# Stick-breaking attention: two query blocks in turn, and the total of later keys carried in one row instead of multiplied

## The chip, the cores and the metric

The kernel runs on one core of one Trainium2 chip. The metric is the device time of one execution in microseconds (us); lower is better. Engine names below are those of the profile: PE is TensorE (PEld its weight loads), DVE VectorE, ACT ScalarE, POOL GpSimd, SP the engine that issues the DMAs.

## The reference

A decoder trunk of two layers on 512 tokens of width 2048 in float32. Layer 0 is an indexer-sparse attention, layer 1 a stick-breaking attention with 16 query heads of 128 that share 4 key/value heads; each layer ends with an output projection, a LayerNorm and a gated per-layer embedding. The change lies in the stick-breaking attention:

```python
def block_fn(args):                      # one block of 128 queries
    z = jnp.einsum('bqngd,bsnd->bngqs', qg, k).astype(jnp.float32) * (HEAD_DIM ** -0.5)
    strict = key_pos[None, :] < t[:, None]
    log_om = jnp.where(strict, -jax.nn.softplus(z), 0.0)
    suffix = lax.cumsum(log_om, axis=log_om.ndim - 1, reverse=True) - log_om
    a = jnp.where(strict, jnp.exp(jax.nn.log_sigmoid(z) + suffix), 0.0)
    o = jnp.einsum('bngqs,bsnd->bqngd', a.astype(v.dtype), v)
```

The weight of key s for query t is sigmoid(z) times the product of 1 − sigmoid(z) over the keys between s and t. In log space the exponent is z minus the sum of softplus(z) over the key itself and all later ones before t.

## The kernel before, in words

Every float32 product is made of three matmuls on values split in a high and a low part (`split`: ACT rounds the high part, DVE subtracts for the low one; `mm3`: high·high, high·low, low·high). Nearly all ACT and DVE instructions go through one wrapper, so that they carry line 111 in the profile; they are told apart by their tiles. The three matmuls of `mm3` are lines 136 to 138.

The order of PE's instructions is the order in which they are written (the schedule of PE is manual); the other engines' order is made by a scheduler when the program is built, except where an instruction is pinned to program order. Each engine works through its order one by one.

The stick-breaking stage runs over four head groups g of four query heads that share a key head. `sticks(g, Q)` treats a group in ten units (i, kb): query block i of 128 queries against key block kb ≤ i of 128 keys, all four heads side by side, so that a tile has 128 keys on its partitions and 4 x 128 = 512 columns. The ten units come in the order (0,0), (1,1), (1,0), (2,2), (2,1), (2,0), (3,3) and so on: of a query block, the latest keys first. Each unit has three steps:

- `logits(u)`: three matmuls give z in one of PSUM banks 4, 5, 6, which take turns (`spare`). ACT makes e = ln(1 + exp(−|z|)) in three passes (tile `wk`), DVE makes softplus sp = max(z, 0) + e. On the diagonal (kb = i) POOL sets the keys that are not strictly earlier to zero (`strict`, line 1230). sp is split into sh and sl. For the next unit of the same query block either these parts themselves stand ready (`later`), or a running sum over the blocks so far (`run`), split into rh and rl by two further DVE operations.
- `weights(u)`: matmuls add onto z in PSUM (line 1272). With `tri`, which is −1 on and below the diagonal, minus the sum over a key and the later ones of its block; with `neg`, which is −1 everywhere, minus the sum over all later blocks of the query block (only where kb < i). ACT takes the exponential, POOL masks it on the diagonal, and it is split into two parts in the tiles `A` (shown as c).
- `values(u)`: three matmuls with V add onto the output of the query block in bank 7; after kb = 0 ACT copies it to F[g] (f<-o).

In step s stand logits(s), weights(s−1) and values(s−2). Between any two of them PE computes part of the next gate projection (tiles g, banks 0 to 3) by `interleave`, whose weights arrive by DMA (raw) and are split by ACT and DVE (wh, wl) meanwhile. At the end of a group four SiLU passes on ACT free banks 0 to 3. `split_scaled(g+1, i)` turns the queries of block i of the next group into their two parts once the present group has read block i for the last time (tiles c<-f).

Of the kernel before, what the change touches and what calls it, by code (L numbers as in the profile page):

```python
# [51 lines left out]
def steps(gen, n):  # L52
    for _ in range(n):
        next(gen, None)
# [23 lines left out]
def trunk_kernel(  # L78
# [17 lines left out]
    pe = nc.tensor  # L96
# [21 lines left out]
    act, dve, pool = (Paced(e) for e in (nc.scalar, nc.vector, nc.gpsimd))  # L118
# [9 lines left out]
    def bank(i, name="ps"):  # L128
        return psum.tile([128, 512], F32, name=name, tag=f"bank{i}")

    def split(hi, lo, src, eng=dve):
        act.activation(hi, src, AF.Copy)
        eng.tensor_tensor(lo, src, hi.bitcast(F32), ALU.subtract)

    def mm3(out, a, b, start, stop):
        pe.matmul(out, a[0], b[0], start=start, stop=False)  # L136
        pe.matmul(out, a[0], b[1], start=False, stop=False)  # L137
        pe.matmul(out, a[1], b[0], start=False, stop=stop)  # L138
# [4 lines left out]
    neg = top.tile([128, 128], F32R, name="neg")  # L143
    tri = top.tile([128, 128], F32R, name="tri")
# [19 lines left out]
    units = []  # L164
# [158 lines left out]
    bg = deque()  # L323
# [386 lines left out]
    for i in range(1, 4):  # L710
        o = (i - 1) * 128 + 64
# [493 lines left out]
    px = pc_.enter_context(ss(name="px", bufs=1))  # L1205

    def split_scaled(g, i):
        qh, ql = (q.rearrange("p (h q) -> p h q", h=4) for q in Q[i])
        src = F[g][:, :, i * 128 : (i + 1) * 128]
        act.activation(qh, src, AF.Copy, scale=HSCALE)  # L1210
        dve.scalar_tensor_tensor(ql, src, HSCALE, qh.bitcast(F32), ALU.mult, ALU.subtract)
# [11 lines left out]
        tc.keep_in_program_order(act.preload_act_table_set("natural_log_exp_and_others"))  # L1223

    def work():
        return px.tile([128, 512], F32, name="wk", tag="wk", bufs=4)

    def strict(ap):
        v = ap.rearrange("p (h q) -> p h q", h=4)
        pool.affine_select(out=v, in_=v, pattern=[[0, 4], [1, 128]], compare_op=ALU.is_gt, fill=0.0, base=0, channel_multiplier=-1)  # L1230

    def sticks(g, Q):
        units = [(i, kb) for i in range(4) for kb in range(i, -1, -1)]
        later = {}
        running = {}
        state = {}
        out = {}

        def logits(u):
            i, kb = units[u]  # L1240
            z = spare("z")
            ks = slice(kb * 128, (kb + 1) * 128)
            mm3(z, [k[:, ks] for k in K[g]], Q[i], True, True)
            e = work()
            keep = kb == i > 1
            sp = px.tile([128, 512], F32, name="run", tag="run", bufs=2) if keep else work()
            act.activation(e, z, AF.Abs)
            act.activation(e, e, AF.Exp, scale=-1.0)
            act.activation(e, e, AF.Ln, bias=1.0)
            dve.scalar_tensor_tensor(sp, z, 0.0, e, ALU.max, ALU.add)  # L1250
            if kb == i:
                strict(sp)
            parts = tuple(px.tile([128, 512], F32R, name=f"s{s}", tag=f"s{s}", bufs=4) for s in "hl")
            split(*parts, sp)
            state[u] = z, parts
            if keep:
                running[i] = sp
            if kb == i:
                later[u + 1] = parts
            elif kb:  # L1260
                below = tuple(px.tile([128, 512], F32R, name=f"r{s}", tag=f"s{s}", bufs=4) for s in "hl")
                dve.tensor_tensor(running[i], running[i], sp, ALU.add)
                dve.tensor_copy(below[0], running[i])
                dve.tensor_tensor(below[1], running[i], below[0].bitcast(F32), ALU.subtract)
                later[u + 1] = below

        def weights(u):
            i, kb = units[u]
            z, parts = state[u]
            terms = [(neg, p) for p in (later[u] if kb < i else ())] + [(tri, p) for p in parts]  # L1270
            for n, (m, p) in enumerate(terms, 1):
                pe.matmul(z, m, p, start=False, stop=n == len(terms), skip_group_check=True)  # L1272
            a = work()
            act.activation(a, z, AF.Exp)
            if kb == i:
                strict(a)
            parts = A[u % 2]
            split(*parts, a)
            state[u] = parts

        def values(u):
            i, kb = units[u]
            if kb == i:
                out[i] = bank(7, "o")
            mm3(out[i], [v[:, g * 128 : (g + 1) * 128] for v in V[kb]], state.pop(u), kb == i, kb == 0)
            if kb == 0:
                act.activation(F[g][:, :, i * 128 : (i + 1) * 128], out[i].rearrange("p (h q) -> p h q", h=4), AF.Copy)

        for s in range(12):

            done = [i for n, (i, kb) in enumerate(units) if kb == 0 and s == max(n + 3, 0 if g else 8)]
# [12 lines left out]
    def after_combining(fn, *args):  # L1304
        with tc.issue_after(combined):
            fn(*args)

    bg.extend(lambda i=i: after_combining(split_scaled, 0, i) for i in range(2))
    banks = mm_banks("g")
    chunk = gate_first(banks)  # L1310
    gemm = pumped(chunk)
    first = sticks(0, Q)
    for n in (9, 1):
        steps(gemm, n)
        steps(first, 1)
    bg.extend(lambda i=i: split_scaled(0, i) for i in (2, 3))
    steps(gemm, 8)
    gemm = pumped(chunk, 2)

    for g in range(4):  # L1320
        if g:
            log_exp()
            banks = mm_banks("g")
            gemm = pumped(gemm_w(items, plain, banks))
        if 0 < g < 3:
            bg.append(lambda g=g: split_keys(g + 1))
        if g:
            interleave(sticks(g, Q), 30 + 4, gemm, 52, lead=8)
        else:
            interleave(first, 30 - 2, gemm, 64 - 18)  # L1330
        drain()
        if g < 3:
            split_scaled(g + 1, 3)
        for h in range(4):
            sg = work()
            act.activation(sg, banks[h], AF.Silu)
            dve.tensor_tensor(F[g][:, h], F[g][:, h], sg, ALU.mult)
# [52 lines left out]
```

## Time and profile before

| what | value |
|---|---|
| median of 3 runs | 1871.95 us (1871.68 to 1872.62) |
| the profiled execution's own time | 1871.96 us |
| its span in the trace | 1870.2 us |
| first to last logits matmul of the stick-breaking stage | 1239.9 to 1480.2 us of the span |
| granted TensorE clock | 1.0 of full speed |

Busy times are unions of the intervals of an engine's instructions. A group line of the profile reads: line, engine, operation, out<-in with buffer numbers left out, shapes, count, then busy us and mean ns of one, then idle time of the engine ahead of them and what ended it. A line of the timeline reads: start, duration, engine, line, operation, operands, count.

### The profile page before, as it was taken

Reading aid. Unit: us, or ns where it says so; the run is one execution under the profiler, and the core shown is the slowest. Engines: PE = TensorE matmul, PEld = TensorE weight load, DVE = VectorE, ACT = ScalarE, POOL = GpSimd, SP = SyncE. Lnnn points to the kernel's source line nnn. Section 1 sums busy time; section 2 is a strip of 40 time slices with the busy share of each in tenths; the row PEclk is TensorE's granted clock in tenths of the full one; section 3 lists DMA queues with packets and bytes.
Section 4 is the critical chain, followed back from the end, with each engine's and each line's share of the span. In section 5 each row is a group of like instructions: output and inputs, shape, how many; then the busy total and the mean of one; then the engine's idle time right before and its main releaser. Section 6 shows DMA issues by size and latency. Waiting matters only on the chain.

```text
span 1870.2 us, 24902 instructions
## 1 busy us (share of the span) xinstructions
PE 1863.4 (100%) x9229; PEld 1586.1 (85%) x9229; DVE 1196.2 (64%) x2326; ACT 940.9 (50%) x1712; POOL 26.8 (1%) x46
## 2 busy tenths in 40 slices
PE   9999999999999999999999999999999999999998
PEld 8898888888888888888888999988888888888887
DVE  5668678566556444675467788877656645567534
ACT  3546333355554432474245444478877743347422
POOL 0000000000000000000000000000100000000000
PEclk9999999999999999999999999999999999999999
DMA  6442333322222532333334333323222253243333
GB/s 197 127 121 61 102 90 102 91 67 68 68 69 59 162 117 79 124 101 102 124 124 124 102 102 102 108 85 90 59 68 69 64 183 100 74 130 94 120 102 113
DMA packets 111178, 189.21 MB, mean 101 GB/s; under 512 B 8528, under 2 KB 29008, under 8 KB 111056
## 3 DMA queue, kind: packets, MB, share of 16 engines
q1 hardware_dynamic: 111056, 187.62, 33.1%
q8 instruction: 72, 1.18, 0.3%
q14 instruction: 50, 0.41, 0.1%
HBM read 179.21 MB, written 8.39 MB: 100 GB/s over the span
## 4 chain that ended last, share of the span: by engine, by line
PE 99%; ACT 0%; DVE 0%; issue 0%; ACTq 0%
PE g L136 12%; PE g L138 12%; PE g L137 12%; PE o L137 7%; PE o L138 7%; PE o L136 7%; PE m L136 4%; PE m L138 4%; PE m L137 4%; PE q L137 3%; PE q L136 3%; PE q L138 3%; PE k L137 2%; PE k L138 2%; PE k L136 2%; PE z L1272 2%
## 5 line engine op out<-in xcount | busy, mean ns | idle before, releaser
L111 ACT ACTIVATE wh<-raw 128x512 fp32r<-128x512 f32 (+3 forms) x685 | 397.9, 582 | 702.0 <-PE g L137 234.1
L111 DVE TENSOR_TENSOR wl<-raw,wh 128x512 fp32r<-128x512 f32 (+3 forms) x685 | 430.9, 630 | 473.7 <-ACT wh L111 458.3
L136 PE MATMUL g<-xh,wh 128*128 128x512 f32 x1024 | 403.7, 394 | 0.1
L138 PE MATMUL g<-xh,wl 128*128 128x512 f32 x1024 | 399.4, 390 | 0.0
L137 PE MATMUL g<-xl,wh 128*128 128x512 f32 x1024 | 399.4, 390 | 0.0
L138 PEld LDWEIGHTS g<-xh,wl 128*128 128x128 f32 x1024 | 192.2, 188 | 40.8
L136 PEld LDWEIGHTS g<-xh,wh 128*128 128x128 f32 x1024 | 192.4, 188 | 38.3 <-ACT wk L111 0.8
L137 PEld LDWEIGHTS g<-xl,wh 128*128 128x128 f32 x1024 | 192.5, 188 | 37.0
L138 PE MATMUL o<-xh,wl 128*128 128x512 f32 x512 | 199.3, 389 | 0.0
L137 PE MATMUL o<-xl,wh 128*128 128x512 f32 x512 | 199.2, 389 | 0.0
L136 PE MATMUL o<-xh,wh 128*128 128x512 f32 x512 | 199.2, 389 | 0.0
L138 PEld LDWEIGHTS o<-xh,wl 128*128 128x128 f32 x512 | 96.1, 188 | 20.2 <-DVE wl L111 0.3
L137 PEld LDWEIGHTS o<-xl,wh 128*128 128x128 f32 x512 | 96.1, 188 | 20.1
L136 PEld LDWEIGHTS o<-xh,wh 128*128 128x128 f32 x512 | 96.1, 188 | 19.9
L136 PE MATMUL q<-xh,wh 128*128 128x512 f32 x256 | 99.6, 389 | 0.0
L137 PE MATMUL q<-xl,wh 128*128 128x512 f32 x256 | 99.6, 389 | 0.0
L138 PE MATMUL q<-xh,wl 128*128 128x512 f32 x256 | 99.6, 389 | 0.0
L111 ACT ACTIVATE sh<-st 128x512 fp32r<-128x512 f32 x80 | 49.7, 624 | 44.4 <-DVE st L111 44.3
L111 DVE TENSOR_TENSOR sl<-st,sh 128x512 fp32r<-128x512 f32 x80 | 55.2, 691 | 13.9 <-ACT sh L111 13.9
L111 DVE TENSOR_TENSOR xl<-f,xh 128x512 fp32r<-128x512 f32 x80 | 54.3, 686 | 12.6 <-ACT f L111 12.3
L111 ACT ACTIVATE wk<-z 128x512 f32<-128x512 f32 x80 | 47.2, 590 | 23.8 <-PE z L138 16.3
L136 PEld LDWEIGHTS q<-xh,wh 128*128 128x128 f32 x256 | 48.0, 188 | 10.1
(289 smaller groups left out, 3340.1 us busy)
## 6 DMA issues: line engine op xcount, KB each, us to landing
raw<-w_in_a SPq DMA_DIRECT2D x95, 512.0 KB, 3.7
raw<-w_in_b SPq DMA_DIRECT2D x64, 512.0 KB, 3.8
raw<-w_ple_gate SPq DMA_DIRECT2D x52, 512.0 KB, 3.7
raw<-w_o_a SPq DMA_DIRECT2D x24, 512.0 KB, 3.8
raw<-w_o_b SPq DMA_DIRECT2D x24, 512.0 KB, 3.7
raw<-w_kv_b SPq DMA_DIRECT2D x16, 512.0 KB, 3.7
raw<-w_ple_gate SPq DMA_DIRECT2D x24, 256.0 KB, 2.9
f<-xT SPq DMA_DIRECT2D x4, 1024.0 KB, 6.5
```

Source lines behind the costliest of these rows:

```text
L111: ins = method(*args, **kw)
L136: pe.matmul(out, a[0], b[0], start=start, stop=False)
L137: pe.matmul(out, a[0], b[1], start=False, stop=False)
L138: pe.matmul(out, a[1], b[0], start=False, stop=stop)
L1272: pe.matmul(z, m, p, start=False, stop=n == len(terms), skip_group_check=True)
```

## The change

The total over later key blocks is no longer multiplied with `neg`. It is written into row 0 of sp, the row of the block's first key, and a second triangular matrix `tri0` has −1 in the whole of the matching row, so that the two triangular matmuls of the unit spread it over all keys. Row 0's own softplus is lost by that, so DVE puts −ln(1 + exp(z)) + z = min(z, 0) − e straight into row 0 of z. The total itself is read off after the triangular matmuls: the first row of z before them minus the first row after them goes to the next unit of the query block (`first`, tile `y`, one partition by 512 columns). On the diagonal this is the sum over the whole block; off the diagonal it is what was carried in plus the block's sum without its first key.

So that this total has time to return, the units of two query blocks alternate, and two units of one query block are two steps apart. z takes turns in banks 4 and 5, and the outputs lie in banks 6 and 7. The pool of `wk` has 5 buffers instead of 4, that of sh and sl 3 instead of 4, `run` is gone, `y` has 3. The query splits follow the new order of the blocks (block 0 last).

```diff
+    tri0 = px.tile([128, 128], F32R, name="tri0")
+    dve.tensor_copy(tri0, tri.bitcast(F32))
+    dve.tensor_copy(tri0[0:1], neg[0:1].bitcast(F32))
+
     def sticks(g, Q):
-        units = [(i, kb) for i in range(4) for kb in range(i, -1, -1)]
-        later = {}
-        running = {}
+        units = [(1, 1), (3, 3), (1, 0), (3, 2), (2, 2), (3, 1), (2, 1), (3, 0), (2, 0), (0, 0)]
+        total = {}
...
-            z = spare("z")
+            z = bank(4 + u % 2, "z")
...
             dve.scalar_tensor_tensor(sp, z, 0.0, e, ALU.max, ALU.add)
+            first = None
+            if kb:
+                first = px.tile([1, 512], F32, name="y", tag="y", bufs=3)
             if kb == i:
+                if kb:
+                    dve.tensor_copy(first, z[0:1])
                 strict(sp)
-            parts = tuple(px.tile([128, 512], F32R, name=f"s{s}", tag=f"s{s}", bufs=4) for s in "hl")
+            else:
+                if kb:
+                    dve.scalar_tensor_tensor(first, z[0:1], 0.0, e[0:1], ALU.min, ALU.subtract)
+                    dve.tensor_copy(z[0:1], first)
+                else:
+                    dve.scalar_tensor_tensor(z[0:1], z[0:1], 0.0, e[0:1], ALU.min, ALU.subtract)
+                dve.tensor_copy(sp[0:1], total.pop(i))
+            parts = tuple(px.tile([128, 512], F32R, name=f"s{s}", tag=f"s{s}", bufs=3) for s in "hl")
             split(*parts, sp)
-            state[u] = z, parts
-            if keep:
-                running[i] = sp
-            if kb == i:
-                later[u + 1] = parts
-            elif kb:
-                below = tuple(px.tile([128, 512], F32R, name=f"r{s}", tag=f"s{s}", bufs=4) for s in "hl")
-                dve.tensor_tensor(running[i], running[i], sp, ALU.add)
-                dve.tensor_copy(below[0], running[i])
-                dve.tensor_tensor(below[1], running[i], below[0].bitcast(F32), ALU.subtract)
-                later[u + 1] = below
+            state[u] = z, parts, first
 
         def weights(u):
             i, kb = units[u]
-            z, parts = state[u]
-            terms = [(neg, p) for p in (later[u] if kb < i else ())] + [(tri, p) for p in parts]
-            for n, (m, p) in enumerate(terms, 1):
-                pe.matmul(z, m, p, start=False, stop=n == len(terms), skip_group_check=True)
+            z, parts, first = state[u]
+            for n, p in enumerate(parts):
+                pe.matmul(z, tri if kb == i else tri0, p, start=False, stop=n == 1, skip_group_check=True)
+            if kb:
+                dve.tensor_tensor(first, first, z[0:1], ALU.subtract)
+                total[i] = first
             a = work()
             act.activation(a, z, AF.Exp)
...
-                out[i] = bank(7, "o")
+                out[i] = bank(7 if i in (0, 3) else 6, "o")
...
-    bg.extend(lambda i=i: after_combining(split_scaled, 0, i) for i in range(2))
+    bg.extend(lambda i=i: after_combining(split_scaled, 0, i) for i in (1, 3))
...
-    bg.extend(lambda i=i: split_scaled(0, i) for i in (2, 3))
+    bg.extend(lambda i=i: split_scaled(0, i) for i in (2, 0))
...
-            split_scaled(g + 1, 3)
+            split_scaled(g + 1, 0)
```

More of the change, by code (lines that the diff above doesn't have):

```diff
@@ L1225, in work @@
     def work():
-        return px.tile([128, 512], F32, name="wk", tag="wk", bufs=4)
+        return px.tile([128, 512], F32, name="wk", tag="wk", bufs=5)
     def strict(ap):
@@ L1244, in logits @@
             e = work()
-            keep = kb == i > 1
-            sp = px.tile([128, 512], F32, name="run", tag="run", bufs=2) if keep else work()
+            sp = work()
             act.activation(e, z, AF.Abs)
@@ L1289, in sticks @@
         for s in range(12):
-            done = [i for n, (i, kb) in enumerate(units) if kb == 0 and s == max(n + 3, 0 if g else 8)]
+            done = [i for n, (i, kb) in enumerate(units) if kb == 0 and s == max(n + 3, 0 if g else 8) and i]
             if g < 3:
```

## The prediction

> **What bounds the kernel now.** I read the page first, then the busy time by stretch over the stage that the change touches, then the groups of instructions in that stage, the waits, and last the timeline around single units.
>
> ```profile
> span 1870.2 us, 24902 instructions
> PE 1863.4 (100%) x9229; PEld 1586.1 (85%) x9229; DVE 1196.2 (64%) x2326; ACT 940.9 (50%) x1712; POOL 26.8 (1%) x46
> ...
> 1300.00:1361.00 61.00, 61.00 (x269) 50.13 (x268) 39.91 (x63) 48.44 (x87) 5.88 (x8) 1.00 0.21 62
> 1361.00:1422.00 61.00, 60.90 (x268) 49.79 (x267) 39.55 (x62) 49.77 (x88) 5.88 (x8) 1.00 0.23 68
> ...
> 1239.70:1490.50 250.80, 250.23 (x1098) 205.16 (x1097) 162.31 (x257) 202.80 (x362) 23.31 (x32) 1.00 0.24 70
> ```
>
> Columns of the last three lines: stretch and length, then busy time (and count) of PE, PEld, DVE, ACT and POOL, the granted clock, and DMA. The stick-breaking stage lies between 1239.7 and 1490.5. PE is busy all of it at full clock, so a PE instruction taken out there saves its time, and a wait put in there costs its time. 268 matmuls in 60.90 us are 0.227 us each; a matmul row of 0.39 us overlaps its neighbours, so 0.227 is the price. ACT is next (49.77 of 61 us, 82%), DVE has 39.55 (65%). The waits in this stage say how little slack PE has:
>
> ```profile
> PEld o L137 <- DVE c L111: 1.1, 3, 0.5
> PEld z L1272 <- DVE sl L111: 0.9, 2, 0.6
> ...
> PEld g L136 <- ACT wk L111: 0.8, 2, 0.5
> ```
>
> (Total, times, longest.) Nearly nothing in 250 us: whatever ACT and DVE must deliver arrives, but the 0.9 on sl shows that in two units it arrives at the last moment.
>
> **What goes.** The matmuls with neg:
>
> ```profile
> L1272 PE MATMUL z<-sh,neg 128*128 128x512 f32 x12 | 4.7, 389 | 0.0
> L1272 PE MATMUL z<-sl,neg 128*128 128x512 f32 x12 | 4.7, 389 | 0.0
> L1272 PE MATMUL z<-rh,neg 128*128 128x512 f32 x12 | 4.7, 389 | 0.0
> L1272 PE MATMUL z<-rl,neg 128*128 128x512 f32 x12 | 4.7, 389 | 0.0
> ...
> L111 DVE TENSOR_TENSOR run<-run,wk 128x512 f32<-128x512 f32 x12 | 11.0, 918 | 0.3
> L111 DVE TENSOR_TENSOR rl<-run,rh 128x512 fp32r<-128x512 f32 x12 | 8.2, 683 | 0.0
> L111 DVE CAST rh<-run 128x512 fp32r<-128x512 f32 x12 | 5.0, 420 | 0.1
> ```
>
> 48 matmuls at 0.227 us are **10.9 us** off PE, 2.7 in each of the four head groups, with no new matmul in their place. The order of all other PE instructions stays, position by position; only the unit that stands at a position is another. The three DVE groups, 24.2 us in all, lay beside PE and save nothing by themselves.
>
> **What comes on DVE.** Per group 24 operations on one partition by 512: six subtractions of z's first row, six of the form min-subtract, three copies of z's row out, three copies into it, six copies of the total into sp. No operation on one partition is in the trace. Bounds:
>
> ```profile
> L111 DVE RECIPROCAL sm<-sm 128x1 f32<-128x1 f32 x64 | 10.3, 161 | 17.7 <-ACT p L111 17.0
> L111 DVE TENSOR_TENSOR f<-rp,sw 32x512 f32<-32x512 f32 x16 | 10.9, 679 | 0.4
> ```
>
> 32 partitions by 512 cost 679 ns, as 128 by 512 do (683 above): the columns set the price, not the partitions. So I take 0.68 for the two-input forms, the upper end, and 0.42 (the CAST) for a copy within SBUF; the lower end is 0.16, a price without columns. A queue of such operations starts one every 0.6 us (below, 1399.58 to 1400.19). Per group that is 18 x 0.6 + 6 x 0.42 = 13.3 us more and 6.1 less: DVE rises from 39.55 to about 46.8 in a stretch that shrinks to 58.3 us, 80%; ACT's share becomes 85%. Neither engine becomes the bound by its sum. What counts is where the new operations stand in the chains.
>
> **What the chains lose.** In each step PE issues logits of unit u (Z), the triangular matmuls of u-1 (W) and the value matmuls of u-2 (V), with gate matmuls between. These are the rows of the third group (from 1370) around the three places that I work out.
>
> ```profile
> 1377.78 0.39 PE L1272 MATMUL z<-sh,tri 128*128 128x512 f32 x1
> 1378.01 0.39 PE L1272 MATMUL z<-sl,tri 128*128 128x512 f32 x1
> 1378.35 0.68 DVE L111 TENSOR_TENSOR sl<-wk,sh 128x512 fp32r<-128x512 f32 x1
> 1378.43 0.60 ACT L111 ACTIVATE wk<-z 128x512 f32<-128x512 f32 x1 [0.21 <-PE z L1272]
> 1378.91 0.39 PE L136 MATMUL z<-c,c 128*128 128x512 f32 x1
> 1379.16 0.64 POOL L1230 TENSOR_SCALAR_AFFINE_SELECT wk<-wk 128x512 f32<-128x512 f32 x1 [1.75 <-ACT wk L111]
> ...
> 1394.78 0.39 PE L138 MATMUL z<-c,c 128*128 128x512 f32 x1
> ...
> 1399.58 0.68 DVE L111 TENSOR_TENSOR sl<-wk,sh 128x512 fp32r<-128x512 f32 x1
> 1400.19 0.68 DVE L111 TENSOR_TENSOR wl<-raw,wh 128x512 fp32r<-128x512 f32 x1
> ...
> 1401.55 0.39 PE L1272 MATMUL z<-rh,neg 128*128 128x512 f32 x1
> 1402.00 0.39 PE L1272 MATMUL z<-sh,tri 128*128 128x512 f32 x1
> ...
> 1415.83 0.39 PE L138 MATMUL z<-c,c 128*128 128x512 f32 x1
> ...
> 1420.72 0.68 DVE L111 TENSOR_TENSOR sl<-wk,sh 128x512 fp32r<-128x512 f32 x1
> 1421.49 0.39 PE L1272 MATMUL z<-sh,tri 128*128 128x512 f32 x1
> ```
>
> *First place: bank of the third unit.* The logits now alternate between two banks where three rotated, so Z of unit 2 must wait until the exponential of unit 0 has read its bank. In the built program that exponential in turn stands behind DVE's subtraction of the same bank's first row, and in groups two to four the subtraction stands behind sl of unit 1 in DVE's queue. W of unit 0 ends at 1378.40; sl of unit 1 starts at 1378.35, so the subtraction runs from 1378.95 to about 1379.63, the exponential from 1379.67 to 1380.27 (it ran from 1378.43 before), and Z of unit 2 starts at 1380.3 instead of 1378.91. **1.4 us per group**, and behind it waits all of PE's queue. In the first group the subtraction stands ahead of sl, which makes it some 0.9 there; I keep 1.4, since that group also carries the restoring copies of the x blocks.
>
> The Trainium skill, PSUM — Partial Sum Buffer, "PSUM bank collisions raise a hardware error", says that ScalarE and VectorE must not touch one bank and quadrant at once, reads against reads included, so that the two have to be put in order. That is what speaks against reading a row and the whole bank after the same matmul; the waits in the built program agree with it, and no run so far shows its price. If they could read side by side, this place would cost some 0.7 less per group and the next 0.5 less, which puts the sum some 5 us lower.
>
> *Second place: the total's way into the triangular product.* A unit off the diagonal now waits between sp and its rounding sh for one or two further DVE operations on row 0: the min-subtract (0.6) and the copy of the total (0.42), 1.0 to 1.1 us with the hand-over. At the sixth position now: last Z at 1394.78, sl done at 1400.26, 5.48 us later; the tri matmul that needs sh comes 7.22 us after Z, and that with sl 0.23 later. Of this allowance 0.45 go with the unit's own neg matmuls and 0.45 with those of the unit before: 6.55 remain to the second. The need grows by 1.1 and by about 0.7 for the exponential of the unit before, which now holds ACT's queue until its subtraction is done, ahead of sh: 7.3. That is **0.8 us of stall**. The other five off-diagonal positions come out, by the same subtraction, between nothing and 0.3, because three of them lost run, rh and rl (2.0 us) out of the DVE queue ahead of sl, and those of the last key block have no subtraction. I take 0.6 for the five: **1.4 per group**. Bounds: nothing, if the slack that the waits view does not show is there everywhere; six times 0.8.
>
> *Third place: the last unit.* Its tri matmul comes 5.66 us after the last Z (1415.83 to 1421.49). Both neg pairs ahead of it go: 4.76, and 4.98 for the one with sl. Now sl is done 5.57 us after Z. The unit that stands there after the change is (0,0), a diagonal one, which sends sp through POOL first (0.64, and some 0.1 for the hand-over): 6.3. **1.3 us per group.** The waits ahead of it stay the same, so this place is the surest.
>
> **Sum.** New stalls 1.4 + 1.4 + 1.3 = 4.1 per group, 16.4 in four. Stalls of now that fall together with them, from the two rows of waits on c and sl: 2.0, of which I take 1.5 off. Query splits: block 0 is now split last instead of block 3, and the second unit of the next group needs block 3; it is split some ten us ahead, so nothing, but one conversion more on ACT ahead of the silu that frees the gate banks, where PE already waited 0.8 in two places: 0.5 more in all. The copies that make tri0 (two in all) stand where DVE combines the last product; the first logits wait for the query split just behind: below 0.3, taken as nothing. SP's queue, its DMAs and POOL's 32 selections stay. So −10.9 + 16.4 − 1.5 + 0.5 = **+4.5 us**. The profiled execution took 1871.96 us, equal to the median 1871.95, so the forecast is **1876.5 us**: slightly slower, just over the 0.2% (3.7 us) that a measurement can tell from no change. Its own range, with each place off by a third: 1871 to 1882. Chance 0.5.
>
> **Rivals.**
> - *Faster: only the unavoidable part stalls.* If DVE and ACT reach each new operation at once, the first place costs 0.85 (subtraction from 1378.42, exponential to 1379.72) and the second nothing. For the third, the bare links are
>
> ```profile
> L111 ACT ACTIVATE wk<-wk 128x512 f32<-128x512 f32 x80 | 50.2, 627 | 1.5
> L111 ACT ACTIVATE wk<-z 128x512 f32<-128x512 f32 x80 | 47.2, 590 | 23.8 <-PE z L138 16.3 <-PE z L1272 7.3
> ...
> L111 DVE SCALAR_TENSOR_TENSOR wk<-z,wk 128x512 f32<-128x512 f32 x32 | 22.1, 689 | 19.2 <-ACT wk L111 19.0
> L111 DVE TENSOR_TENSOR sl<-wk,sh 128x512 fp32r<-128x512 f32 x32 | 21.9, 685 | 3.4 <-ACT sh L111 3.4
> ...
> L111 ACT ACTIVATE sh<-wk 128x512 fp32r<-128x512 f32 x32 | 19.9, 622 | 1.3 <-DVE wk L111 0.9 <-POOL wk L1230 0.4
> ```
>
> the matmul's 0.39, abs 0.59, exp and ln 1.25, sp 0.69, select 0.64, sh 0.62, sl 0.69, together 4.9, and some 0.3 of hand-overs: 5.2 against 4.98 leaves 0.3 to 0.6. That is 1.3 a group, 5.2 in all: −10.9 − 1.5 + 5.2 = −7.2, **1864.8 us**. For it: the order of DVE and ACT has been made anew for this program, and a PE that stalls gives both engines time. Against it: in the built order sl of unit 1 and a weight split stand ahead of those very operations. It decides where the stalls stay under 2.3 us a group. Cheaper row operations (0.16) would lead here too. Chance 0.27.
> - *Clearly slower: ACT becomes the pace.* Six exponentials per group hold ACT for the subtraction, 0.7 each, 4.2 us; with 49.8 of 58.3 us ACT has 8.5 left, most of it where PE has not yet delivered Z. If the delays add up instead of hiding in these gaps, each of the six off-diagonal units pays the 0.8 of the sixth: 1.4 + 4.8 + 1.3 = 7.5 per group, 30 in all: +18, **1890 us** at worst, 1885 with half of it hidden. Chance 0.18.
> - *The change brings nothing because PE's time is not the sum of its matmuls.* If the neg matmuls ran where PE would have waited anyway, their removal gives nothing and the stalls still come. Against it: the four neg groups show no idle time before them. Chance 0.05; 1880 to 1887.
>
> **How the numbers follow.** The forecast's own range lies a little over half above 1875.7 and the rest within 0.2%; the first rival is mostly below 1868.2. So faster 0.26, same 0.23, slower 0.51. The range takes the first rival's time and the middle of the second: 1864 to 1886.
>
> **What would show it.** In the profile after: no neg rows and 48 PE instructions fewer; small DVE groups y, z and wk of 1x512 at 0.6 to 0.7 us; in the waits, PE or PEld z waiting for ACT (the third unit) at 1 us or more four times, PEld z waiting for DVE sl at the last unit four times. The stage from first to last z would be some 245 + 16 − 11 us long, a few us longer than now. I am wrong if PE's waits in the stage stay under 9 us (then it is faster), if the 1x512 operations take 0.2 us, or if the exponentials do not wait for DVE.

## The result, and the profile after

The changed kernel takes **1884.7 us** (1884.61 to 1884.78, four runs) against 1871.86 us (1871.68 to 1872.62, four runs) of the kernel before: a ratio of 1.0068, with a 95% interval of 1.005 to 1.0085. It is 12.8 us slower where 4.5 were forecast. The profiled execution took 1884.70 us.

Two lines of the page of after, and then the busy time by stretch over the whole stage (columns as in the prediction):

```profile
span 1883.0 us, 24868 instructions
...
PE 1861.9 (99%) x9181; PEld 1575.2 (84%) x9181; DVE 1225.8 (65%) x2388; ACT 945.1 (50%) x1712; POOL 28.2 (1%) x46
```

```profile
1239.70:1503.00 263.30, 248.52 (x1050) 194.03 (x1049) 192.16 (x319) 207.17 (x362) 24.72 (x32) 1.00 0.22 66
```

The 48 matmuls are gone (9229 to 9181), yet the stage takes 263.3 us instead of 250.8, and PE has no row in 14.8 of them, where it had none in 0.6. The clock is full as before. DVE is busy 73% and ACT 79% of the stage, so neither became the bound by its sum.

The groups of the new operations on one partition, in the stage:

```profile
L111 DVE TENSOR_TENSOR y<-y,z 1x512 f32<-1x512 f32 x24 | 16.1, 672 | 8.2 <-PE z L1278 8.2
...
L111 DVE COPY wk<-y 1x512 f32<-1x512 f32 x24 | 10.0, 416 | 0.0
...
L111 DVE COPY z<-y 1x512 f32<-1x512 f32 x12 | 8.1, 674 | 0.0
```

With three more groups of 12, of 669 to 683 ns, these are 96 operations and 58.4 us. Anything that touches PSUM costs 0.67 to 0.68 us, copies too; only the copy from y into wk within SBUF costs 0.42. The waits of the stage (total, times, longest):

```profile
PEld z L1278 <- DVE sl L111: 11.7, 18, 1.4
PEld z L136 <- ACT wk L111: 9.8, 8, 2.0
DVE y L111 <- PE z L1278: 8.2, 12, 1.5
ACT wk L111 <- DVE y L111: 7.9, 11, 1.3
...
PE z L136 <- ACT wk L111: 6.9, 5, 1.6
...
PE z L1278 <- DVE sl L111: 4.6, 10, 1.1
```

The first row answers to the 0.9 us of before: PE's triangular matmuls now wait for sl 18 times. The rows with ACT wk are the logits that wait until an exponential has read their bank, and the two rows with y show why that is late: the subtraction waits for the triangular matmuls, the exponential for the subtraction.

A busy share hides part of PE's stalls, since a matmul's row lasts 0.39 or 0.50 us and the next should start 0.227 after it. So I add up by how much neighbouring starts in the stage lie further apart than 0.227 (without the places where one record is missing). That gives PE's stalls by place: 2.2 us before, **24.7 us after**. 22.5 more stalls less 10.9 us of matmuls make +11.6; the remaining 1.2 of the 12.8 lies outside the gaps counted so. In the rest, Z2 is the first logits matmul of the group's third unit, W9 the triangular matmuls of the last unit (units are counted from 0), V9 its value matmuls. This is Z2 in the third group, on the timeline of after:

```profile
1383.87 0.67 DVE L111 COPY y<-z 1x512 f32<-1x512 f32 x1
1384.02 1.61 POOL L1230 TENSOR_SCALAR_AFFINE_SELECT wk<-wk 128x512 f32<-128x512 f32 x1 [1.85 <-DVE wk L111]
...
1384.47 0.67 DVE L111 TENSOR_TENSOR sl<-wk,sh 128x512 fp32r<-128x512 f32 x1
...
1385.65 0.39 PE L1278 MATMUL z<-sl,tri 128*128 128x512 f32 x1
...
1385.67 0.63 ACT L111 ACTIVATE sh<-wk 128x512 fp32r<-128x512 f32 x1 [0.32 <-POOL wk L1230]
...
1386.33 0.69 DVE L111 TENSOR_TENSOR sl<-wk,sh 128x512 fp32r<-128x512 f32 x1 [0.15 <-ACT sh L111]
1386.94 0.67 DVE L111 TENSOR_TENSOR y<-y,z 1x512 f32<-1x512 f32 x1
1387.64 0.60 ACT L111 ACTIVATE wk<-z 128x512 f32<-128x512 f32 x1 [1.34 <-DVE y L111]
...
1388.30 0.50 PE L136 MATMUL z<-c,c 128*128 128x512 f32 x1 [1.58 <-ACT wk L111]
...
1388.63 0.40 PE L137 MATMUL z<-c,c 128*128 128x512 f32 x1
```

The triangular matmuls of unit 0 end at 1386.04. DVE then still has sl of unit 1 to do, subtracts at 1386.94, ACT takes the exponential at 1387.64, and PE's logits start at 1388.30; without the stall they were due about 1386.56, 0.227 after the matmul of 1386.33. sl is late since sh waits for POOL (0.32), whose mask of unit 1 takes 1.61 us here (1384.02), beside the saved row (1383.87) and the sl of unit 0 behind it. In the kernel before, without the saved row, sl comes earlier beside the mask, and the same mask of the same position took 1.03; in both kernels it ends 0.5 after that sl:

```profile
1376.23 0.68 DVE L111 TENSOR_TENSOR sl<-wk,sh 128x512 fp32r<-128x512 f32 x1
1376.38 1.03 POOL L1230 TENSOR_SCALAR_AFFINE_SELECT wk<-wk 128x512 f32<-128x512 f32 x1 [1.84 <-DVE wk L111]
```

And this is the last unit of the third group, on the timeline of after:

```profile
1428.23 0.68 DVE L111 SCALAR_TENSOR_TENSOR wk<-z,wk 128x512 f32<-128x512 f32 x1
...
1428.98 0.64 POOL L1230 TENSOR_SCALAR_AFFINE_SELECT wk<-wk 128x512 f32<-128x512 f32 x1 [20.44 <-DVE wk L111]
...
1429.65 0.63 ACT L111 ACTIVATE sh<-wk 128x512 fp32r<-128x512 f32 x1
...
1430.34 0.49 PE L1278 MATMUL z<-sh,tri 128*128 128x512 f32 x1 [0.41 <-ACT sh L111]
1430.37 0.69 DVE L111 TENSOR_TENSOR sl<-wk,sh 128x512 fp32r<-128x512 f32 x1
...
1431.11 0.50 PE L1278 MATMUL z<-sl,tri 128*128 128x512 f32 x1 [0.28 <-DVE sl L111]
...
1432.37 0.63 POOL L1230 TENSOR_SCALAR_AFFINE_SELECT wk<-wk 128x512 f32<-128x512 f32 x1 [2.75 <-ACT wk L111]
...
1434.19 0.69 DVE L111 TENSOR_TENSOR c<-wk,c 128x512 fp32r<-128x512 f32 x1 [0.65 <-ACT c L111]
...
1434.94 0.50 PE L137 MATMUL o<-c,c 128*128 128x512 f32 x1 [0.23 <-DVE c L111]
```

PE waits for sh (0.41) and for sl (0.28), counted from the end of the row before; by the starts it is 1.23 in all. Then, as the unit is a diagonal one, POOL masks the exponential as well (1432.37), and the value matmul with c's low part waits again (0.23, some 0.6 with its surroundings).

The groups take 70.1, 67.5 and 67.2 us from first logits to first logits, against 65.2, 65.0 and 64.6 before: 5.0 more in the first group, 2.5 in each of the next.

### The profile page after: what moved, and what is told of

Read it like the earlier page. It is cut to its first block, busy times and chain, and to the rows that moved or that the text cites. A ratio compares the mean times of both kernels' runs of the same rounds, so it can differ in the third digit from the quotient of the medians.

```text
span 1883.0 us, 24868 instructions
## 1 busy us (share of the span) xinstructions
PE 1861.9 (99%) x9181; PEld 1575.2 (84%) x9181; DVE 1225.8 (65%) x2388; ACT 945.1 (50%) x1712; POOL 28.2 (1%) x46
## 5 line engine op out<-in xcount | busy, mean ns | idle before, releaser
L111 DVE TENSOR_TENSOR sl<-st,sh 128x512 fp32r<-128x512 f32 x80 | 55.1, 690 | 13.9 <-ACT sh L111 13.9
L137 PEld LDWEIGHTS q<-xl,wh 128*128 128x128 f32 x256 | 48.0, 188 | 10.1
```

Of the source, the lines that this page charges most:

```text
L111: ins = method(*args, **kw)
```

## The experiments

The table gives PE's stalls by place for a ladder from before to after; the experiments behind its columns follow. All in us.

| place | before | count_only | no_rows | no_subtract | after |
|---|---|---|---|---|---|
| Z2, bank of the third unit | 0 | 0 | 1.65 | 2.01 | 6.55 |
| W2 to W8, total's way | 0.67 | 2.57 | 0.59 | 3.23 | 7.63 |
| Z3, Z5, Z7 | 0 | 0 | 0 | 0 | 2.02 |
| W9, last unit | 0 | 2.11 | 4.93 | 5.83 | 4.56 |
| V9, its values | 0 | 0 | 2.59 | 2.58 | 2.59 |
| other (V0, V3, gate after SiLU) | 1.56 | 2.91 | 1.33 | 1.4 | 1.38 |
| sum | 2.2 | 7.6 | 11.1 | 15.0 | 24.7 |
| time | 1871.9 | 1866.7 | 1870.8 | 1875.6 | 1884.7 |

**count_only**: the kernel before without the neg matmuls.

```diff
-            terms = [(neg, p) for p in (later[u] if kb < i else ())] + [(tri, p) for p in parts]
+            terms = [(tri, p) for p in parts]
```

> The kernel before with the matmuls of neg left out and nothing else changed (the later blocks' share of the exponent is missing from the output). If PE's time is the sum of its matmuls, 48 x 0.227 = 10.9 us go: 1861.0 us, or up to 2 us more if the last unit of a group, whose allowance shrinks by 0.9 us, now waits for sl. If the neg matmuls only filled time in which PE would have waited, nothing goes: 1871 to 1872.

Measured 1866.69 us (1866.48 to 1867.14), ratio 0.9973 (0.9962 to 0.9983): 5.4 faster, half of the 10.9 that the matmuls are worth. The waits of this run show where the other half went:

```profile
PEld z L1272 <- DVE sl L111: 4.0, 8, 1.1
...
PEld o L137 <- DVE c L111: 2.5, 3, 1.0
```

The neg matmuls were also the time in which ACT and DVE brought the parts. Without them PE comes to the same places earlier, and its stalls rise from 2.2 to 7.6, by just the 5.4 that are missing. DVE still makes run, rh and rl here, though nobody reads rh and rl. To leave out the multiplication, and nothing else, is worth 5.4.

**no_rows**: after, without any operation on row 0 (tri for tri0). What is left is the count of matmuls, the order of the units and the banks; the DVE operations for run, rh and rl are gone as well.

```diff
...
-                    dve.tensor_copy(first, z[0:1])
...
-                    dve.scalar_tensor_tensor(first, z[0:1], 0.0, e[0:1], ALU.min, ALU.subtract)
-                    dve.tensor_copy(z[0:1], first)
-                else:
-                    dve.scalar_tensor_tensor(z[0:1], z[0:1], 0.0, e[0:1], ALU.min, ALU.subtract)
-                dve.tensor_copy(sp[0:1], total.pop(i))
...
-                pe.matmul(z, tri if kb == i else tri0, p, start=False, stop=n == 1, skip_group_check=True)
-            if kb:
-                dve.tensor_tensor(first, first, z[0:1], ALU.subtract)
-                total[i] = first
+                pe.matmul(z, tri, p, start=False, stop=n == 1, skip_group_check=True)
```

> The changed kernel without any operation on row 0: no y, no min-subtract, no copy of the total, tri in place of tri0 (the output lacks the share of the later blocks). What is left of the change is the order of the units, two banks for z and 48 matmuls fewer. Theory (chains): the third unit still waits 0.9 a group, the last unit 1.2 for its tri matmuls and 0.6 for its values, 10 to 12 us of stalls in all against 10.9 us saved: 1869 to 1873, so that half of the loss has nothing to do with the rows. Rival (the rows are the whole loss): all stalls go and 10.9 us are gained, 1861.

Measured 1870.78 us (1870.41 to 1871.05), ratio 0.9993 (0.9984 to 1.0003). It is 4.1 us above count_only, and the row operations add 13.9 more. The 4.1 hold what the new order and the two banks cost, and against it whatever no_rows gains because the 36 DVE operations for run, rh and rl (24.2 us), which count_only still does, are gone; no run separates the two. W9 and V9 are there in full without a single row operation.

**no_subtract**: after, without the subtraction; the total handed on is the first row as it was saved.

```diff
-                dve.tensor_tensor(first, first, z[0:1], ALU.subtract)
                 total[i] = first
```

> The changed kernel without the 24 subtractions that read z's first row after the triangular matmuls; the row that was read before them is passed on instead (the output lacks most of the total). Theory (chains): the exponential waits for PE alone; the third unit's stall falls from 1.85 to about 0.9 a group, that at the sixth position to nearly nothing, and in the first group those before its sixth and seventh unit (1.75 and 1.5) shrink: 7 to 10 us less, 1875 to 1878. Rival (added DVE work as such): 24 of 96 row operations are gone and 24.2 of some 57 us of added work came back already, so 2 to 3 us less, 1882.

Measured 1875.57 us (1874.96 to 1875.82), ratio 1.0019 (1.0009 to 1.0028): taken out of after, these 24 subtractions give 9.1 of the 13.9, and 4.8 are left with the 72 other operations. Z2 falls to 2.01. The weight loads' wait of the logits for ACT, 9.8 us in after, falls to this:

```profile
PEld z L136 <- ACT wk L111: 2.6, 4, 1.0
```

**exp_first**: after, with the exponential ahead of the subtraction.

```diff
+            a = work()
+            act.activation(a, z, AF.Exp)
             if kb:
                 dve.tensor_tensor(first, first, z[0:1], ALU.subtract)
                 total[i] = first
-            a = work()
-            act.activation(a, z, AF.Exp)
```

> The changed kernel with the exponential written ahead of DVE's subtraction, so that the subtraction waits for the exponential and not the other way round. Theory (chains): the third unit's bank is still held until both have read it, but ACT no longer stands still; the stalls at the sixth position (some 0.8 in each group) and half a us of each 1.85 us at the third unit go: 4 to 6 us less, 1879 to 1881. Rival (the added DVE work as such sets the pace): the work is the same, 1884 to 1885.

Measured 1882.41 us (1882.12 to 1883.11), ratio 1.0057 (1.0042 to 1.0072): 2.3 faster than after, short of what was expected. The exponential waits for DVE no more, but now the subtraction is the last reader of the bank, and PE waits for it instead:

```profile
PEld z L136 <- DVE y L111: 9.5, 9, 2.0
```

So turning the order of the two reads gives 2.3 of the 9.1. The traces show three ways in which the subtraction can cost, and this run keeps each in part; how the 9.1 divide among them isn't shown: a bank that is free late, a place in DVE's queue, and the idle time in which DVE stands at its head until PE is done (DVE y waiting for PE, 8.2 us in after).

**third_bank**: after, with the third unit in bank 7.

```diff
-            z = bank(4 + u % 2, "z")
+            z = bank(7 if u == 2 else 4 + u % 2, "z")
```

> The changed kernel with z of the third unit in bank 7, which is free at that time, so that this unit need not wait for the exponential of the first. Theory (the bank is what holds the third unit): the stalls there (1.0 + 3 x 1.85 us) go, and at most 0.5 us a group come up where the first values of block 3 now want bank 7: 4.5 to 6.5 us less, 1878 to 1880. Rival (the delay is passed on: what the third unit no longer waits, the next triangular matmuls wait, since ACT and DVE deliver no sooner): 1883 to 1885.

Measured 1882.23 us (1881.82 to 1882.83), ratio 1.0053 (1.0038 to 1.0068). Z2 is gone, 6.55 to nothing, but only 2.5 are gained: the delay sits in the exponential, and the next that needs it are the first two value steps.

```profile
PEld o L137 <- DVE c L111: 5.0, 8, 0.9
...
PEld o L136 <- ACT c L111: 4.1, 8, 0.9
```

V0 and V1, which had no stall in after, have 5.01 and 2.36 here.

**tail_fill** gives the last unit more gate matmuls ahead of its weights and values, taken from the rest of the group; **tail_before** does the same to the kernel before.

```diff
+                if (s, fn) in ((9, values), (10, weights)):
+                    yield
...
-            interleave(sticks(g, Q), 30 + 4, gemm, 52, lead=8)
+            interleave(sticks(g, Q), 30 + 6, gemm, 55, lead=5)
...
-            interleave(first, 30 - 2, gemm, 64 - 18)
+            interleave(first, 30, gemm, 64 - 18)
```

> The changed kernel with gate matmuls moved inside each group: three of the eight steps that stood ahead of a group's first logits, and two more places for them, one ahead of the last unit's triangular matmuls and one ahead of the last two value products. No work is added or taken away. Theory (the last unit's chain has too short an allowance): of the 4.6 us ahead of the last triangular matmuls and the 2.6 us in the last values most go: 5 to 7 us less, 1878 to 1880. Rival (ACT and DVE are behind throughout, so the stall moves to another place): 1883 to 1885.

> The kernel before with the same move of gate matmuls to the end of each group, to see whether the move alone gains. Its PE waits only some 2 us in the whole stage and little of it at the last unit: 1871 to 1872.5 by the theory. If the move shortens something that no wait shows, it is faster by 1 us or more.

Measured 1881.29 us (1881.02 to 1881.6), ratio 1.0048 (1.0033 to 1.0063), and 1873.25 us (1872.9 to 1873.86), ratio 1.0006 (0.9996 to 1.0016): 3.4 faster than after, and 1.2 above the kernel before as it was timed beside it (1872.09), which the interval does not tell from no change. V9 went, W9 did not (4.7): in the order that was made anew, ACT takes a weight split ahead of sh of the last unit, as the timeline of tail_fill shows.

```profile
1425.67 0.64 POOL L1230 TENSOR_SCALAR_AFFINE_SELECT wk<-wk 128x512 f32<-128x512 f32 x1 [20.54 <-DVE wk L111]
...
1426.35 0.64 ACT L111 ACTIVATE wh<-raw 128x512 fp32r<-128x512 f32 x1
...
1426.89 0.61 ACT L111 ACTIVATE sh<-wk 128x512 fp32r<-128x512 f32 x1
```

The mask is done at 1426.31, and sh could start there; it starts at 1426.89. W2 rose as well, from 2.0 to 4.89; that its step gave up gate matmuls would explain it, but no run shows that by itself. In the kernel before, which has no such stall, the move brings nothing.

**all_three**: exp_first, third_bank and tail_fill together.

> The changed kernel with the exponential ahead of the subtraction, the third unit in bank 7 and the gate matmuls moved to the end of a group. Theory: of the 22.4 us of stalls that the kernel with the exponential first has, 5.5 at the third unit and 6 of 7.2 at the last go: 1882.4 - 11.5 = 1871, level with the kernel before; 1869 to 1873. Rival (stalls move on): 1876 or more.

Measured 1880.38 us (1879.99 to 1880.62), ratio 1.0043 (1.0028 to 1.0058). The single gains, 2.3, 2.5 and 3.4, would add to 8.2; 4.3 came. The stalls (20.5) are again elsewhere: W2 4.99, W9 4.12, Z6 3.51. Z6 is one stall of the first group, with 2.97 us from start to start (1269.34 to 1272.32), and the matmuls behind it: in this execution the granted clock is at half for the 3.41 us from 1271.9, so that they start 0.43 apart, and some 1.4 of the 20.5 are this and no wait. With this the idea of three places with a price each, each to be mended by itself, fell: a stall that is taken away at one place comes back, in good part, at another.

**rows_idle**: no_rows with as many operations on one partition as after has, 24 a group, which nobody reads. They are written behind the split of sp, but need only sp and e; the scheduler, which makes DVE's order, put those of the unit shown below ahead of sl.

```diff
             split(*parts, sp)
-            state[u] = z, parts, first
+            for _ in range(3 if kb == i else 2):
+                y = px.tile([1, 512], F32, name="y", tag="y", bufs=3)
+                dve.tensor_tensor(y, sp[0:1], e[0:1], ALU.subtract)
+            state[u] = z, parts
```

> The kernel of no_rows with 24 subtractions of 1x512 on DVE per head group put back, as many as the changed kernel has operations on row 0, but on rows of SBUF that nothing reads: the load is there, the chains are not (the output lacks the share of the later blocks). Theory (the chains cost, not the load): 1870.8 plus at most 2 us, since two such operations stand ahead of each sl: 1871 to 1873. Rival (DVE's load sets the pace): most of the 14 us between no_rows and the changed kernel come back: 1880 or more.

Measured 1886.98 us (1885.63 to 1890.39), ratio 1.0082 (1.0067 to 1.0097): 16.2 slower than no_rows and even above after, although no engine waits for a result of these operations. Its last unit, third group:

```profile
1429.69 0.63 ACT L111 ACTIVATE sh<-wk 128x512 fp32r<-128x512 f32 x1
1429.69 1.89 DVE L111 TENSOR_TENSOR y<-wk 1x512 f32<-1x512 f32 x3 [0.80 <-POOL wk L1230]
...
1431.50 0.67 DVE L111 TENSOR_TENSOR c<-wk,c 128x512 fp32r<-128x512 f32 x1
1432.10 0.67 DVE L111 TENSOR_TENSOR sl<-wk,sh 128x512 fp32r<-128x512 f32 x1
...
1432.83 0.50 PE L1268 MATMUL z<-sl,tri 128*128 128x512 f32 x1 [1.96 <-DVE sl L111]
```

sh is ready at 1430.32, but DVE is at the three operations until 1431.58 and then takes c; sl starts 1.78 us after sh is ready, where it starts 0.09 after it in the last unit of after (1430.28 and 1430.37, above). PE waits 1.96. The busy time by stretch, then the waits:

```profile
1239.70:1505.00 265.30, 248.62 (x1054) 195.98 (x1053) 200.68 (x320) 204.18 (x362) 27.74 (x32) 0.99 0.22 66
```

```profile
PEld z L1268 <- DVE sl L111: 18.7, 20, 2.4
```

DVE is busy 200.7 of 265.3 us, 76%. The share of busy time doesn't show this loss; the wait shown here comes from what stands in an in-order queue ahead of the one operation that PE needs next.

Two other things are in the 16.2. The mean clock of the stage is 0.99: it is at half from 1298.3 to 1301.7, just behind a stall of 2.36 us from start to start. Of the four executions, the one at full clock took 1885.63 (14.9 above no_rows) and the one with the lowest clock, 0.997, took 1890.39. And these operations read SBUF alone, where most of the real ones read or write PSUM: POOL's 32 masks take 27.7 us here and 22.1 in no_rows. What that costs PE no run shows.

**rows_late**: the same number of idle operations, but behind the split of the weights.

```diff
+            for _ in range(3 if kb == i else 2):
+                y = px.tile([1, 512], F32, name="y", tag="y", bufs=3)
+                dve.tensor_tensor(y, parts[0][0:1].bitcast(F32), parts[1][0:1].bitcast(F32), ALU.subtract)
```

> The kernel of no_rows with the same number of idle subtractions of 1x512 on DVE as rows_idle (24 per head group), written behind the split of the weights instead of behind softplus, reading the parts of that split; the scheduler puts them behind the split, before or behind the sl of the next unit (the output lacks the share of the later blocks). The theory of pure dependencies fell with rows_idle (1886.98). Left are two: DVE's place (an operation costs where it stands between a unit's softplus and its sl in the queue): there are fewer of these here, none at a group's last unit, 1872 to 1877. DVE's load (each of the 96 costs some 0.17 us wherever it stands): 1884 to 1888.

Measured 1879.26 us (1878.25 to 1879.72), ratio 1.0038 (1.0023 to 1.0052): 8.5 above no_rows, more than was expected of operations at this place.

```profile
PEld z L1265 <- DVE sl L111: 13.2, 14, 2.5
```

They do not stand behind everything. The scheduler put one of them ahead of sl even at the last unit of the third group, where the expectation had none:

```profile
1426.95 0.49 PE L1265 MATMUL z<-sh,tri 128*128 128x512 f32 x1 [0.47 <-ACT sh L111]
1427.04 0.68 DVE L111 TENSOR_TENSOR y<-c 1x512 f32<-1x512 f32 x1
1427.64 0.67 DVE L111 TENSOR_TENSOR sl<-wk,sh 128x512 fp32r<-128x512 f32 x1
...
1428.37 0.50 PE L1265 MATMUL z<-sl,tri 128*128 128x512 f32 x1 [0.93 <-DVE sl L111]
```

Moving them halves the price but doesn't take it away: about 0.09 us for each operation here, 0.16 to 0.17 in rows_idle, 0.14 for the real ones (13.9 over 96). So the place in the queue counts, though POOL's masks differ too (27.7 us in rows_idle, 23.2 here); whether the mere number counts isn't shown, since places ahead of sl remain here. How the 13.9 of the real ones divide into waits for their results and time in the queue stays open: idle operations at a bad place, whose results nobody awaits, reach as much.

**diagonal_earlier**: no_rows with another order, in which block 3 runs with block 2 and block 1 with block 0, so that (0,0) is the last but one and (1,0) last; the query splits follow it.

```diff
-        units = [(1, 1), (3, 3), (1, 0), (3, 2), (2, 2), (3, 1), (2, 1), (3, 0), (2, 0), (0, 0)]
+        units = [(3, 3), (2, 2), (3, 2), (2, 1), (3, 1), (2, 0), (3, 0), (1, 1), (0, 0), (1, 0)]
...
+            split_scaled(g + 1, 1)
```

> The kernel of no_rows with another order of the units, in which block 3 runs with block 2 and block 1 with block 0, so that the last unit of a group is (1,0), off the diagonal and without the selection on POOL (the output lacks the share of the later blocks). Theory (the last unit's chain is too long by the selection): of its 1.24 us ahead of the triangular matmuls and 0.6 us ahead of the values most of 0.7 each goes, 3 to 5 us in four groups: 1866 to 1868. Rival (the chain is held up by other work ahead of it): 1870 to 1871.

Measured 1865.97 us (1865.69 to 1866.23), ratio 0.9967 (0.9954 to 0.998): 4.8 faster than no_rows. W9 falls from 4.93 to 0.94, V9 to nothing, and W8, now the diagonal unit's, has 2.96. So most of what no_rows stalls at the end of a group goes when the diagonal unit stands elsewhere. As this order changes the other positions too, the 4.8 are not the price of that unit alone, and what the two banks cost isn't separated either: Z2 keeps its 1.65. Whether this order would help after itself, with its row operations, wasn't tried.

**neg_high**: the kernel before, but the total is multiplied with its high part alone: 24 matmuls and the DVE operations for rl go.

```diff
-            terms = [(neg, p) for p in (later[u] if kb < i else ())] + [(tri, p) for p in parts]
+            terms = [(neg, p) for p in (later[u][:1] if kb < i else ())] + [(tri, p) for p in parts]
...
-                dve.tensor_tensor(below[1], running[i], below[0].bitcast(F32), ALU.subtract)
```

> [...] count_only lost half of its saving because the allowances shrink by 0.9 us; here they shrink by 0.45 and DVE has less to do: 5.4 us saved, 0.5 to 2 lost: 1867 to 1868.5. If the loss came from something else than the allowances, it could be the full half: 1869.5.

Measured 1868.09 us (1867.62 to 1868.44), ratio 0.9979 (0.997 to 0.9989): 4.0 faster than before, of the 5.4 that 24 matmuls are worth; PE's stalls rise to 3.4. Of the versions that still carry the total over later blocks it is the fastest, though it leaves out the total's low part. It takes 12 operations off DVE besides, where the change took 36 off and put 98 on (2326 to 2388 in the page).

## Why the prediction was right or wrong

The direction was right, and the outline of the mechanism too: the matmuls went, and PE's new stalls took more than they gave. Two of the three places came out near their size; one was mis-sized and a fourth was missed. The size was off by 8.2 us. Step by step:

- **What goes, 10.9 us.** Right for PE's work. As a gain it is 5.4, since count_only has the stalls that the shorter cover uncovers; the prediction counted these in the second and third place, as a loss of allowance.
- **Prices on DVE.** 0.68 for the two-input forms: measured 0.67 to 0.68. 0.42 for a copy within SBUF: 0.42. DVE's load was not mis-sized, and 0.16 was not near.
- **First place, 1.4 a group.** Measured 1.85 in groups two to four and 0.99 in the first, 6.55 against 5.6. The chain was right, link by link. In groups two to four it is longer: in the third, sl of unit 1 starts 0.68 after W's second matmul where it had started 0.34 after it, since POOL's mask ahead of it grew from 1.03 to 1.61 us; the prediction moved no instruction of POOL and looked for no change there. And a PE that has stalled starts its next matmul 0.33 instead of 0.227 later, some 0.11 that no step had.
- **Second place, 1.4 a group.** Right in groups two to four: the sixth position has 0.80 as forecast, W2 and W7 0.63 against 0.6. Wrong in the first group, which was set equal to the others: there W2, W3, W5, W6, W8, Z3 and Z5 take 5.2 us. The copies that restore the x blocks stand in the same queues (what they cost, no run shows by itself), and the subtraction stands behind the softplus and the saved row of another unit:

```profile
1263.67 0.50 PE L1278 MATMUL z<-sl,tri 128*128 128x512 f32 x1
...
1264.13 0.69 DVE L111 SCALAR_TENSOR_TENSOR wk<-z,wk 128x512 f32<-128x512 f32 x1 [0.52 <-ACT wk L111]
...
1264.74 0.67 DVE L111 COPY y<-z 1x512 f32<-1x512 f32 x1
...
1265.34 0.67 DVE L111 TENSOR_TENSOR y<-y,z 1x512 f32<-1x512 f32 x1
```

The matmul of the unit ends at 1264.17, the subtraction starts 1.17 later. In all, the second place has 9.65 where 5.6 were forecast: **this is the term that was mis-sized most**, by 4.0. The prediction named those copies and left 0.5 for them in the first place, nothing in the second.
- **Third place, 1.3 a group.** Measured 1.22 to 1.23 in three groups, 0.89 in the first; 4.56 against 5.2. It was called the surest, and it was. no_rows has 4.93 there without any row operation, so it needs none.
- **A place that was missed: the last values, 0.6 a group, 2.6 in all.** The prediction followed the diagonal unit to its sl and no further. It passes POOL a second time, after the exponential. From its last triangular matmul's start to the start of the operation that makes c's low part it takes 3.08 us (1431.11 to 1434.19 above), against 2.18 in the unit that stood there before:

```profile
1421.72 0.39 PE L1272 MATMUL z<-sl,tri 128*128 128x512 f32 x1
...
1423.90 0.68 DVE L111 TENSOR_TENSOR c<-wk,c 128x512 fp32r<-128x512 f32 x1
```

- **Old stalls, −1.5, and query splits, +0.5.** The stalls on c went, 0.9 in V0 and V3. Those on sl, 0.67 in W6 and W8 of the first group, are still there and larger; they stand in the second place's 9.65, and the sum below books the whole 1.5 as gone. The gates behind the SiLU passes have 1.38 instead of 0.67.
- **The sum.** First +0.95, second +4.05, third −0.64, missed +2.6, splits +0.2: 7.1 us over the forecast's stalls, and 1.2 that the gaps don't hold.
- **The rivals.** "Only the unavoidable part stalls" fell: every group stalls far above 2.3 us. "PE's time is not the sum of its matmuls" holds by half, as count_only showed. That the neg groups had no idle time before them spoke against it and was true, but it doesn't follow that their removal is a gain in full: other matmuls then wait. "ACT becomes the pace" had a time near the measured one, 1885, by another way: the six off-diagonal units do not pay 0.8 each, and ACT has 56 us free in the stage. What it did see, delays that add up instead of hiding, is what all_three and the idle rows show, in the idle rows on DVE. Its 1885 does not follow from its own terms either: with half of its 4.8 a group hidden the sum gives some 1880. In the first rival, 5.2 against 4.98 leaves 0.2 and not 0.3 to 0.6, and the +0.5 of the query splits is left out; both move 1864.8 by 1 us at most.
- **The length of the stage.** The prediction starts from 245 us from first to last z, where the table ahead of it has 240.3. Counted by the starts of the matmuls, it grew from 240.1 (1240.16 to 1480.24) to 251.7 (1240.30 to 1492.01), by 11.6; by its terms, 16.4 less 10.9, it was to grow by 5.5.
- **The range** of 1864 to 1886 holds 1884.7; the forecast's own range, 1871 to 1882, does not. The upper end comes from the rival with ACT, which is not what happened, so that the range reaches 1884.7 is luck.

On the Trainium skill, PSUM — Partial Sum Buffer, "PSUM bank collisions raise a hardware error": ScalarE's and VectorE's reads of one bank and quadrant have to be put in order. The trace agrees so far that the two reads stand in order here, in each of the 11 waits of ACT wk for DVE y, 7.9 us. Without the second read the kernel is 9.1 us faster (no_subtract), with the two reads turned 2.3; what the order alone costs isn't shown. That the two could read side by side wasn't tried.

## What to carry to other kernels

Work that is taken off the engine that sets the pace is worth its time only so far as the others keep up: the matmuls removed were cover for two queues, and half of their worth was gone before anything was added. A small operation can cost by what stands behind it in its engine's queue, which neither its length nor the engine's share of busy time shows; ask for each one which operation that the pace-setter needs next it pushes back. And look at the first turn of a loop by itself, and follow a moved unit to its last step, not only to the first late one.

## What the runs showed of the hardware

- An operation of DVE on one partition by 512 columns costs as much as on 128 partitions (0.67 to 0.68 against 0.68 to 0.69 us); a copy on one partition takes 0.67 with PSUM at either end and 0.42 within SBUF. Two idle ones in a row take 1.28 us, three 1.89.
- After a stall PE starts its second matmul 0.33 us after the first (1388.30 and 1388.63 above) instead of 0.227, so that each stall costs some 0.11 us more than the wait that is shown.
- POOL's mask of 128 x 512 mostly took 0.64 us, and 1.61 in the second unit of groups two to four of after, where two DVE operations run beside it; in no_rows, without the saved row, that unit's took 1.03. In the first group the mask of 1.61 is that of the first unit's exponential (1249.81), beside two query splits on DVE. The Trainium skill, SBUF — State Buffer, "Who interferes with whom", has a DVE operation with both inputs in SBUF contend with a GpSimd one that reads SBUF, and lets the order of issue decide which of them blocks. The mask's end 0.49 us after sl's (1385.63 against 1385.14) agrees with the blocking; that its record starts 0.45 ahead of sl's and it still gives way isn't what the order of issue would suggest, and no run here settles it.
- Idle DVE operations cost 0.09 us (rows_late) or 0.16 to 0.17 us (rows_idle) of the kernel's time each, as a mean of 96; DVE was busy 76% of the stage in rows_idle.
- Two traces have a stretch of 3.41 us at half clock in this stage, in which matmuls start 0.43 us apart: all_three from 1271.9, during a stall of PE of 2.97 us from start to start, and rows_idle from 1298.3, behind one of 2.36. Other stalls of 2.46 (rows_idle) and 2.61 (rows_late) have none, so what decides it stays open.
